# Attention with shared key heads on one core: VectorE's add and AND ahead of the copy of the transposes, and three-block jobs from the ninth on

## The chip, the core and the metric

The kernel runs on one core of a Trainium2 chip. The metric is the device time of one execution in microseconds (us). The engines have these names in the profile: PE is TensorE's matmul queue and PEld its weight loads, DVE is VectorE, ACT is ScalarE, POOL is GpSimd, SP is SyncE, which issues the stores.

## The reference

Q is (8, 512, 32, 64): batch, sequence, heads, head size. K and V are (8, 512, 8, 64): each of the 8 key heads serves 4 query heads.

```python
scores = np.einsum('bhqd,bhkd->bhqk', Q, K_expanded) * scale          # scale = 1/8
weights = np.exp(scores - np.max(scores, axis=-1, keepdims=True))
weights = weights / (np.sum(weights, axis=-1, keepdims=True) + 1e-10)
output = np.einsum('bhqk,bhkd->bhqd', weights, V_expanded)
```

The kernel leaves out the subtraction of the maximum and divides after the second product: a column of ones beside V gives the row sums. A flag computed from the sums and from V's largest value says at the end whether that was safe; a general path behind it runs only if it was not.

## The kernel before, in words

**Jobs.** The work is cut into 64 jobs, numbered j = 0 to 63. A job is one batch and one key head with its 4 query heads, held as 2 pairs (`NPAIR`; a pair's two heads lie in the two halves of the partitions, index m). Two jobs in a row (g = 0 and 1) share one load of Q, called u = j // 2. The scores of a job are 16 blocks, each of 128 keys by the 512 queries of one head: 2 pairs x 4 key chunks (kc) x 2 (m). The order of all instructions is written out by hand: each engine runs its own in the order in which the loop over j issues them.

**The exponential is shared out.** Most blocks go to ScalarE: `act_tile(j, n)` puts two blocks into a tile of PSUM (`s_ps`, two buffers) with two matmuls (L208) and turns them into f16 weights with one activation of 1024 columns (L226). The first two blocks of the second pair go to VectorE instead; in a wide job (`WIDE(j)`, taken(j) = 3) the first three do, and one ScalarE tile of the job then has only 512 columns. Either way a job has 7 activations. In the kernel before, the wide jobs are j = 10, 12, ... 62.

**VectorE's share of a job** is a chain over two jobs and two engines. `exp_d` (L237) writes the integer `u` from the scores in `d_ps`, `exp_d2` takes the low bits `f` with an AND (L258), GpSimd makes the correction in two instructions (`g`, L250, then `w`, L254), and in the next job `exp_d4` adds `u` and `w` into the weights `pt` (L271). `by_pool(j)`, true for j = 3 to 62, says that GpSimd makes the correction; for the other jobs VectorE does it all. The first two blocks of `u` are made at the head of the job itself, a third one at the end of the job ahead, in the second bank of the tile that holds the transposes.

**The d_ps tile.** The pool `dps` has one buffer of two banks. It is used twice per job: first for the two score blocks of `exp_d`, then, behind `norm(last, 0)`, for the transposes of Q for a later job (`trans_q`, 8 small matmuls on L172) in bank 0. In a wide job bank 1 then holds the half tile of ScalarE; in the first batch it holds the transposes of K (`first_k`). VectorE copies the transposes to SBUF (`qt`, L176, and `kt_first`, L146). The matmuls that write the next use of `d_ps` wait until the copy has read it. `apart` tells the framework that two accesses touch different banks of one tile, so that it puts no wait between them.

**Transposes ahead.** Job j transposes Q for j + 1 while j < 7; job 7 does so for 8 and 9, in the two banks, and later jobs for j + 2.

**The second product and the division.** Job j computes the second product of job j - 1 (`pv(last, ...)`, L302, 32 small matmuls per pair into a single-buffered `pv` tile), in pieces between the score tiles. Pair 0 comes first; `norm(last, 0)` divides (reciprocal L345, product with broadcast L349). Pair 1 may start when the division of pair 0 has read the `pv` tile; its `blocks` order is kc = 2, 3, 1, 0, so that VectorE's blocks (kc 0 and, in a wide job, the first of kc 1) come last. `cut` says where the pieces of pair 1 end: (11, 19) in a narrow job, (4, 18) in a wide one. Of VectorE's own order in a job, the part that matters is: `u`, for odd j the check of V (L182), division of pair 0, copy of the transposes, add, check of the sums (L313, in every eighth job), AND, third `u` block if the next job is wide, division of pair 1.

**Queues.** POOL issues the loads of Q, K and V (L126, L103, L111) at the head of a job, ahead of that job's correction. SP issues the stores and the transposing copies of K.

Of the kernel before, what the change touches and what calls it, by code (L numbers as in the profile page):

```python
# [33 lines left out]
V_HI = 1.0e15  # L34


WIDE = lambda j: j >= 10 and j % 2 == 0


@with_exitstack  # L40
# [18 lines left out]
def fast_path(ctx, tc, Q, K, V, out, flag):  # L59
    nc = tc.nc  # L60
# [39 lines left out]
    def load_k(b, lo=0, hi=KV):  # L100
        if b not in kn:
            kn[b] = knat_pool.tile([128, SC, KV, D], BF16, name="k_nat")
        nc.gpsimd.dma_start(  # L103
            out=kn[b][:, :, lo:hi, :],
            in_=K[b, :, lo:hi, :].rearrange("(sc p) g d -> p sc g d", p=128),
        )


    def load_v(b, lo=0, hi=KV, chunks=range(SC)):
        for sc in chunks:  # L110
            nc.gpsimd.dma_start(  # L111
                out=vt[b % 2][:, sc, lo:hi, 0:D],
                in_=V[b, sc * 128:(sc + 1) * 128, lo:hi, :],
            )
# [6 lines left out]
    def load_q(u, cuts=(0, 2 * HPG)):  # L121
        b, gp = divmod(u, GP)
        h0 = gp * 2 * HPG
        qn[u] = qnat_pool.tile([128, SC, 2 * HPG, D], BF16, name="q_nat")
        for lo, hi in zip(cuts[:-1], cuts[1:]):
            nc.gpsimd.dma_start(  # L126
                out=qn[u][:, :, lo:hi, :],
                in_=Q[b, :, h0 + lo:h0 + hi, :].rearrange("(sc p) h d -> p sc h d", p=128),
            )

    def d_tile():
        return d_pool.tile([128, 2, S], FP32, name="d_ps")
# [15 lines left out]
    def dma_k(b):  # L148
        kt[b] = kt_pool.tile([128, 2, GP, S], BF16, name="kt")
        for sc in range(SC):  # L150
            nc.sync.dma_start_transpose(
                out=kt[b][:, 0, :, sc * 128:(sc + 1) * 128],
                in_=kn[b][:, sc, :, :].rearrange("p g d -> p (g d)"),
            )
        for to, of in ((0, 64), (64, 0)):
            nc.sync.dma_start(out=kt[b][to:to + 64, 1, :, :], in_=kt[b][of:of + 64, 0, :, :])

    def apart(this, other):
        if other is not None:
            tc.declare_no_dep(  # L160
                this.ins, other.ins, reason="the two are in different banks of one tile"
            )
        return this

    def trans_q(j, bank, lo=0, hi=NPAIR, other=None):
        u, g = divmod(j, 2)
        ps = bank.bitcast(BF16).rearrange("p (i sc c) -> p i sc c", i=NPAIR, sc=SC)
        for i in range(lo, hi):
            for sc in range(SC):
                h = g * HPG + 2 * i  # L170
                apart(
                    nc.tensor.transpose(ps[:, i, sc, :], qn[u][:, sc, h:h + 2, :], ident), other  # L172
                )
        if u not in qt:
            qt[u] = qt_pool.tile([128, 2, NPAIR, S], BF16, name="qt")
        return lambda: apart(nc.vector.tensor_copy(  # L176
            out=qt[u][:, g, lo:hi, :], in_=ps[:, lo:hi, :, :].rearrange("p i sc c -> p i (sc c)")
        ), other)
# [11 lines left out]
    DPAIR = NPAIR - 1  # L190

    def taken(j):
        return 3 if WIDE(j) else 2

# [9 lines left out]
    def scores(j, ps, i, kc, m):  # L204
        u, g = divmod(j, 2)
        b, gp = divmod(u, GP)
        keys = kt_first[:, gp, :, :] if b == 0 else kt[b][:, :, gp, :]
        nc.tensor.matmul(  # L208
            ps,
            keys[64 * m:64 * m + 64, g ^ m, kc * 128:(kc + 1) * 128],  # L210
            qt[u][64 * m:64 * m + 64, g, i, :],
            start=True,
            stop=True,
        )

    def open_job(j):
        pt = pt_pool.tile([128, NPAIR, SC, 2, S], FP16, name="pt")
        jobs.setdefault(j, {}).update(pt=pt, pv={})

    def act_tile(j, n, spare=None):  # L220
        group = act_tiles(j)[n]
        i, kc, lo = group[0]
        ps = s_pool.tile([128, 2, S], FP32, name="s_ps") if spare is None else spare
        for _, _, m in group:
            scores(j, ps[:, m, :], i, kc, m)
        return nc.scalar.activation(  # L226
            out=jobs[j]["pt"][:, i, kc, lo:, :], in_=ps[:, lo:, :], func=EXP, scale=scale
        )

    def exp_d(j, lo, hi, ps):  # L230
        st = jobs.setdefault(j, {})
        if "u" not in st:
            for name, dtype in (("u", I16), ("f", I16), ("g", BF16), ("w", BF16)):
                st[name] = dve_pool.tile([128, 3, S], dtype, name=name + "16")[:, 0:taken(j), :]
        for n in range(lo, hi):
            scores(j, ps[:, n - lo, :], DPAIR, n // 2, n % 2)
        return lambda: nc.vector.tensor_scalar(  # L237
            out=st["u"][:, lo:hi, :], in0=ps[:, 0:hi - lo, :], scalar1=A_U, scalar2=B_U,
            op0=ALU.mult, op1=ALU.add,
        )  # L240


    def by_pool(j):
        return 3 <= j < NJOB - 1
# [23 lines left out]
    def exp_d4(j):  # L268
        st = jobs[j]
        n = taken(j)  # L270
        nc.vector.tensor_tensor(  # L271
            out=st["pt"][:, DPAIR, :, :, :].rearrange("p kc m q -> p (kc m) q")[:, 0:n, :].bitcast(
                U16
            ),
            in0=st["u"],
            in1=st["w"],
            op=ALU.add,
        )
# [132 lines left out]
    bank = d_tile()  # L411
# [4 lines left out]
    bank = d_tile()  # L416
# [3 lines left out]
    for j in range(NJOB):  # L420
        end = j == NJOB - 1
        last = j - 1
        late = last >= 0
        u, g = divmod(j, 2)
        b, gp = divmod(u, GP)
        open_job(j)
        if j == 1:

            nc.gpsimd.tensor_copy(out=gate, in_=jobs[0]["pt"][0:1, 0, SC - 1, 0, 0:1])
            load_q(2)  # L430
            load_q(3)
        if g == 0 and u >= 1 and u + 3 < NU:
            load_q(u + 3)
        if (gp, g) == (1, 0) and b + 1 < B:
            load_k(b + 1)
        if 3 <= 2 * gp + g < 3 + SC and b + 1 < B:
            load_v(b + 1, chunks=(2 * gp + g - 3,))
        if gp == 2 and g == 0 and b + 1 < B:
            dma_k(b + 1)

        cut = (4, 18) if taken(j) > 2 else (11, 19)
        act_tile(j, 0)
        if j == 0:
            trans_q(0, bank[:, 1, :], 1, NPAIR)()
            act_tile(j, 1)
            exp_d(j, 0, 2, d_tile())()
        else:
            exp_d(j, 0, 2, d_tile())()
            act_tile(j, 1)

        if j == 8:
            check_v(0, 0)
        if g == (b < B - 1) and j > 1:
            check_v(b, gp)
        if late:
            pv(last, 0, 0, 16)
        act_tile(j, 2)
        if late:
            pv(last, 0, 16, 32)
            norm(last, 0)  # L460
        act_tile(j, 3)

        reads = []
        if not end:
            bank = d_tile()
            beside = act_tile(j, 4, bank) if taken(j) > 2 else None

            ahead = (j + 1,) if j < 7 else (8, 9) if j == 7 else (j + 2,)
            for n, to in enumerate(ahead):
                if to < NJOB:  # L470
                    reads.append(trans_q(to, bank[:, n, :], other=beside))
            if j == 1:
                for swap in range(2):
                    reads.append(first_k(1, swap, bank[:, 1, swap * S // 2:]))
            elif j > 1 and b == 0 and gp + 1 < GP:
                reads.append(first_k(gp + 1, g, bank[:, 1, :]))
        else:
            pv(j, 0, 0, 16)
        for read in reads:
            read()  # L480

        if late and by_pool(last):
            exp_d4(last)
        check_sums()
        exp_d2(j)
        if not by_pool(j):
            exp_d3(j, nc.vector)
            exp_d4(j)
        if taken(j) == 2:
            act_tile(j, 4)  # L490
        if late:
            pv(last, 1, 0, cut[0])
        act_tile(j, 5)
        if not end and taken(j + 1) > 2:
            exp_d(j + 1, 2, taken(j + 1), bank[:, 1:2, :])()
        if late:
            pv(last, 1, *cut)
        act_tile(j, 6)
        if late:
            pv(last, 1, cut[1], 32)  # L500
            norm(last, 1)
            del jobs[last]
        if end:
            pv(j, 0, 16, 32)
            norm(j, 0)
            pv(j, 1, 0, 32)
            norm(j, 1)
# [118 lines left out]
```

## Time and profile before

| | |
|---|---|
| median of 3 runs | 422.61 us (421.35 to 422.84) |
| profiled execution | 421.88 us, of which the span from first to last instruction is 420.1 us |
| mean granted TensorE clock | 0.987 |
| busy shares | ACT 96%, PE 91%, DVE 83%, POOL 70% |
| ScalarE's exponentials on `s_ps` | 421 instructions of 1024 columns, 393.2 us busy |
| HBM traffic | 50.33 MB read, 33.55 MB written, 200 GB/s over the span |

Rows of the timeline read: start (us), duration (us), engine, line, operation, output tile <- input tiles, how many instructions the row joins, and in square brackets the idle time just before them with what ended it. Successive instructions of one kind are joined, so a row's duration can hold small gaps; activations overlap their successors, so starts say more than durations. The 7 activations of each job make the clock by which the loop can be followed: job 22 has its first at 150.93 us, job 23 at 156.84 us.

### The profile page before, as it was taken

The page shows a single profiled execution, that of the slowest core. Times are in us where ns is not written, and L with a number is a line of the kernel's source. Part 1 is how long each engine was busy: PE and PEld are TensorE (multiplying, and loading weights), DVE is VectorE, ACT ScalarE, POOL GpSimd, SP SyncE. Part 2 cuts the span into 40 slices and gives each one's busy share as a digit, 9 for nine tenths or more (in the row PEclk, how much of TensorE's full clock was granted, in tenths as well). Part 3 has the DMA queues.
Part 4 walks back from the last instruction along what each step waited for, and adds up shares of the span by engine and source line. Part 5 has one row for each costly group of instructions (what it writes and reads, how often), then busy time and mean ns, then how long its engine had stood idle before and what let it go on. Part 6 is the DMA issues. An engine that isn't in the chain of part 4 may idle for free.

```text
span 420.1 us, 13063 instructions
## 1 busy us (share of the span) xinstructions
PE 382.4 (91%) x5689; PEld 232.7 (55%) x5689; DVE 350.1 (83%) x611; ACT 402.2 (96%) x449; POOL 292.3 (70%) x209
## 2 busy tenths in 40 slices
PE   6889999999999999999999999999999999999993
PEld 2456565555555555555555555555555555555552
DVE  2697878888888888898888898888889888988875
ACT  3899999999999999999999999999999999999992
POOL 8504656689758886788866977778875888676560
PEclk9799999999999999999999999999999999999997
DMA  9996985499966998599983999649996799842223
GB/s 98 178 138 156 221 167 138 75 195 188 214 152 88 222 198 160 142 176 152 213 180 102 213 145 249 185 64 200 203 191 151 100 212 200 167 131 101 103 99 107
DMA packets 91438, 66.95 MB, mean 159 GB/s; under 512 B 52080, under 2 KB 74608, under 8 KB 91376
## 3 DMA queue, kind: packets, MB, share of 16 engines
q0 software_dynamic: 56544, 25.17, 52.6%
q1 hardware_dynamic: 34832, 40.90, 33.3%
q8 instruction: 45, 0.74, 0.7%
q14 instruction: 17, 0.14, 0.1%
HBM read 50.33 MB, written 33.55 MB: 200 GB/s over the span
## 4 chain that ended last, share of the span: by engine, by line
ACT 61%; PE 26%; DVE 9%; issue 1%; POOL 1%; ACTq 0%; DVEq 0%; POOLq 0%
ACT pt L226 61%; PE pv L302 11%; PE s_ps L208 10%; PE d_ps L172 3%; DVE o_sb L349 2%; DVE pt L271 2%; DVE u L237 1%; DVE ok L313 1%; PE d_ps L208 1%; DVE f L258 1%; DVE qt L176 1%; DVE w L254 1%; POOL q_nat L126 0%; DVE kt_first L146 0%; PE d_ps L143 0%
## 5 line engine op out<-in xcount | busy, mean ns | idle before, releaser
L226 ACT ACTIVATE pt<-s_ps 128x1024 f16<-128x1024 f32 x421 | 393.2, 1124 | 9.2 <-PE s_ps L208 9.1
L302 PEld LDWEIGHTS <-pt 128*128 128x128 f16 x4096 | 144.1, 98 | 87.8 <-issue 53.6
L302 PE MATMUL pv<-v,pt 128*128 128x65 bf16 x4032 | 183.4, 195 | 8.1 <-DVE pt L271 4.2
L254 POOL TENSOR_TENSOR w<-g,f 128x1024 bf16<-128x1024 bf16 (+1 forms) x60 | 153.9, 2565 | 5.0
L208 PE MATMUL s_ps<-qt,kt 64*128 64x512 bf16 x730 | 142.8, 384 | 15.1 <-ACT pt L226 9.7
L250 POOL TENSOR_SCALAR g<-f 128x1024 bf16<-128x1024 int16 (+1 forms) x60 | 74.0, 1234 | 107.4 <-DVE f L258 107.4
L237 DVE TENSOR_SCALAR u<-d_ps 128x1024 int16<-128x1024 f32 (+1 forms) x91 | 96.2, 1057 | 0.6 <-PE d_ps L208 0.6
L349 DVE TENSOR_TENSOR o_sb<-pv,inv 128x512 f32<-128x512 f32 x125 | 86.5, 692 | 4.5 <-DVE inv L345 0.2
L208 PEld LDWEIGHTS <-kt 64*128 64x128 bf16 x896 | 47.9, 93 | 55.4 <-issue 29.4
L345 DVE RECIPROCAL inv<-pv 128x8 f32<-128x8 f32 x125 | 25.9, 207 | 40.1 <-PE pv L302 39.7
L271 DVE TENSOR_TENSOR pt<-u,w 128x1536 uint16<-128x1536 int16 (+1 forms) x64 | 51.1, 799 | 4.7 <-POOL w L254 3.0
L176 DVE COPY qt<-d_ps 128x1024 bf16<-128x1024 bf16 (+1 forms) x65 | 44.3, 683 | 8.9 <-PE d_ps L172 6.9
L208 PE MATMUL d_ps<-qt,kt 64*128 64x512 bf16 x166 | 41.9, 375 | 0.3
L172 PE MATMUL d_ps<-ident,q_nat 128*128 128x128 bf16 x512 | 40.4, 223 | 1.0 <-DVE kt_first L146 0.9
L172 PEld LDWEIGHTS <-q_nat 128*128 128x128 bf16 x512 | 29.5, 99 | 20.9 <-issue 20.9
L258 DVE TENSOR_SCALAR f<-u 128x1536 int16<-128x1536 int16 (+1 forms) x64 | 30.8, 481 | 0.0
L111 POOL DMA_DIRECT2D v<-in_V_dram x32 | 29.0, 911 | 0.5 <-DMA v<-in_V_dram 0.5
L126 POOL DMA_DIRECT2D q_nat<-in_Q_dram x34 | 27.4, 808 | 1.8 <-DMA q_nat<-in_Q_dram 1.6
L208 PE MATMUL s_ps<-qt,kt_first 64*128 64x512 bf16 x112 | 23.0, 406 | 4.7 <-ACT pt L226 3.8
L182 DVE TENSOR_REDUCE okv<-v 128x1 f32<-128x512 bf16 x32 | 21.6, 676 | 0.0
L226 ACT ACTIVATE pt<-d_ps 128x512 f16<-128x512 f32 x27 | 18.5, 685 | 0.0
L208 PEld LDWEIGHTS <-kt_first 64*128 64x128 bf16 x128 | 7.9, 94 | 12.4 <-issue 8.5
(41 smaller groups left out, 45.3 us busy)
## 6 DMA issues: line engine op xcount, KB each, us to landing
out_dram<-o_sb SPq DMA_DIRECT2D x31, 1024.0 KB, 6.8
q_nat<-in_Q_dram POOLq DMA_DIRECT2D x31, 512.0 KB, 6.1
k_nat<-in_K_dram POOLq DMA_DIRECT2D x7, 512.0 KB, 8.7
v<-in_V_dram POOLq DMA_DIRECT2D x28, 128.0 KB, 7.2
kt<-kt SPq DMA_DIRECT2D x14, 256.0 KB, 4.8
out_dram<-o_sb SPq DMA_DIRECT2D x4, 256.0 KB, 2.4
kt<-k_nat SPq DMA_TRANSPOSE x28, 5.6
v<-in_V_dram POOLq DMA_DIRECT2D x4, 96.0 KB, 8.4
```

The source lines that it names most:

```text
L111: nc.gpsimd.dma_start(out=vt[b % 2][:, sc, lo:hi, 0:D], in_=V[b, sc * 128:(sc + 1) * 128, lo:hi, :],)
L172: nc.tensor.transpose(ps[:, i, sc, :], qn[u][:, sc, h:h + 2, :], ident), other
L176: return lambda: apart(nc.vector.tensor_copy(out=qt[u][:, g, lo:hi, :], in_=ps[:, lo:hi, :, :].rearrange("p i sc c -> p i (sc c)")), other)
L208: nc.tensor.matmul(ps, keys[64 * m:64 * m + 64, g ^ m, kc * 128:(kc + 1) * 128], qt[u][64 * m:64 * m + 64, g, i, :], start=True, stop=True,)
L226: return nc.scalar.activation(out=jobs[j]["pt"][:, i, kc, lo:, :], in_=ps[:, lo:, :], func=EXP, scale=scale)
L237: return lambda: nc.vector.tensor_scalar(out=st["u"][:, lo:hi, :], in0=ps[:, 0:hi - lo, :], scalar1=A_U, scalar2=B_U, op0=ALU.mult, op1=AL ...
L250: engine.tensor_scalar(out=g, in0=f, scalar1=-EXP_F1, scalar2=EXP_K * 2.0 ** (24 * as_bits), op0=ALU.add, op1=ALU.mult,)
L254: engine.tensor_tensor(out=w, in0=g, in1=f.bitcast(FP16) if as_bits else f, op=ALU.mult)
L258: nc.vector.tensor_single_scalar(out=st["f"], in_=st["u"], scalar=1023, op=ALU.bitwise_and)
L271: nc.vector.tensor_tensor(out=st["pt"][:, DPAIR, :, :, :].rearrange("p kc m q -> p (kc m) q")[:, 0:n, :].bitcast(U16), in0=st["u"], in1=st ...
L302: nc.tensor.matmul(st["pv"][i][:, m, qc, :], st["pt"][:, i, kc, m, qc * 128:(qc + 1) * 128], vt[b % 2][:, kc, 2 * gp + g, :], start=(n < 2 ...
L349: nc.vector.tensor_tensor(out=osb[u][:, :, h:h + 2, :].rearrange("p qc m d -> p m qc d"), in0=sums[:, :, :, 0:D], in1=inv[:, :, :, None].t ...
```

## The change

Four edits go together.

- `WIDE` begins at j = 8 instead of 10, so that job 8 is wide too: its third block is computed at the end of job 7.
- Job 6 transposes Q for jobs 7 and 8, and job 7 only for 9; before, job 6 did so for 7, and job 7 for 8 and 9. That leaves bank 1 free in job 7 for the third block of job 8.
- In the jobs with `by_pool(j)` the copies of the transposes move behind the add of the last job, the check of the sums and the AND of this job. In the other jobs (0 to 2 and 63) they stay where they were.
- The score matmul of the third block is declared apart from the copy of the transposes (`copies[0]`), which lies in the other bank; otherwise it would wait for that copy.

```diff
-WIDE = lambda j: j >= 10 and j % 2 == 0
+WIDE = lambda j: j >= 8 and j % 2 == 0
...
-        nc.tensor.matmul(
+        return nc.tensor.matmul(
...
-    def exp_d(j, lo, hi, ps):
+    def exp_d(j, lo, hi, ps, other=None):
...
         for n in range(lo, hi):
-            scores(j, ps[:, n - lo, :], DPAIR, n // 2, n % 2)
+            apart(scores(j, ps[:, n - lo, :], DPAIR, n // 2, n % 2), other)
...
-            ahead = (j + 1,) if j < 7 else (8, 9) if j == 7 else (j + 2,)
+            ahead = (j + 1,) if j < 6 else (7, 8) if j == 6 else (j + 2,)
...
-        for read in reads:
-            read()
-
+        copies = [] if by_pool(j) else [read() for read in reads]
         if late and by_pool(last):
             exp_d4(last)
         check_sums()
         exp_d2(j)
         if not by_pool(j):
             exp_d3(j, nc.vector)
             exp_d4(j)
+        else:
+            copies = [read() for read in reads]
...
-            exp_d(j + 1, 2, taken(j + 1), bank[:, 1:2, :])()
+            exp_d(j + 1, 2, taken(j + 1), bank[:, 1:2, :], copies[0])()
```

## The prediction

> **What bounds the kernel now.** I read the busy shares first, then the stretches of equal length, then ScalarE's timeline alone, then all engines over two jobs, and last the list of who waited for whom.
>
> ```profile
> PE 382.4 (91%) x5689; PEld 232.7 (55%) x5689; DVE 350.1 (83%) x611; ACT 402.2 (96%) x449; POOL 292.3 (70%) x209
> 160.00:210.00 50.00, 47.01 (x709) 28.44 (x708) 43.64 (x75) 49.99 (x57) 38.59 (x26) 1.00 0.96 169
> ```
>
> The second row is a stretch of 50 us: length, sum, then busy time of PE, PEld, DVE, ACT and POOL, granted clock, DMA share, GB/s. ScalarE is busy for 49.99 of 50 us at a clock of 1.00. Read as it stands, only less work for ScalarE could help. But its activations overlap, so a late start can hide in a longer busy time. The starts tell:
>
> ```profile
> 62.68 13.86 ACT L226 ACTIVATE pt<-s_ps 128x1024 f16<-128x1024 f32 x15
> 76.24 1.22 ACT L226 ACTIVATE pt<-s_ps 128x1024 f16<-128x1024 f32 x1
> 79.86 0.84 ACT L226 ACTIVATE pt<-d_ps 128x512 f16<-128x512 f32 x1
> 80.33 12.28 ACT L226 ACTIVATE pt<-s_ps 128x1024 f16<-128x1024 f32 x13
> 154.55 0.66 ACT L226 ACTIVATE pt<-d_ps 128x512 f16<-128x512 f32 x1
> 155.03 12.10 ACT L226 ACTIVATE pt<-s_ps 128x1024 f16<-128x1024 f32 x13
> 403.25 0.67 ACT L226 ACTIVATE pt<-d_ps 128x512 f16<-128x512 f32 x1
> 161.36 1.18 ACT L226 ACTIVATE pt<-s_ps 128x1024 f16<-128x1024 f32 x1
> 162.40 1.06 ACT L226 ACTIVATE pt<-s_ps 128x1024 f16<-128x1024 f32 x1
> ```
>
> From 62.68 to 76.24 us, 15 full tiles start 13.56/15 = 0.904 us apart: ScalarE's own pace. A half tile is followed after 0.48 us (154.55 to 155.03). So a wide and a narrow job together need 13 x 0.904 + 0.48 = 12.23 us. The half tiles mark these pairs: from 79.86 to 403.25 us there are 26 of them, 323.39/26 = 12.44 us each. So 0.206 us per pair, 26 x 0.206 = **5.36 us** in all, is time in which a full ScalarE had no tile ready. The place is the last tile of the narrow job: in job 23 it starts 162.40 - 161.36 = 1.04 us after the one before, 0.14 late. Why:
>
> ```profile
> 153.37 0.69 DVE L349 TENSOR_TENSOR o_sb<-pv,inv 128x512 f32<-128x512 f32 x1
> 154.21 0.69 DVE L176 COPY qt<-d_ps 128x1024 bf16<-128x1024 bf16 x1 [0.16 <-PE d_ps L172]
> 154.82 0.68 DVE L271 TENSOR_TENSOR pt<-u,w 128x1024 uint16<-128x1024 int16 x1
> 155.42 0.55 DVE L258 TENSOR_SCALAR f<-u 128x1536 int16<-128x1536 int16 x1
> 156.07 1.47 POOL L250 TENSOR_SCALAR g<-f 128x1536 bf16<-128x1536 int16 x1 [1.40 <-DVE f L258]
> 156.39 0.39 PE L208 MATMUL d_ps<-qt,kt 64*128 64x512 bf16 x2
> 157.62 3.10 POOL L254 TENSOR_TENSOR w<-g,f 128x1536 bf16<-128x1536 bf16 x1
> 159.27 0.69 DVE L349 TENSOR_TENSOR o_sb<-pv,inv 128x512 f32<-128x512 f32 x1
> 159.91 0.69 DVE L176 COPY qt<-d_ps 128x1024 bf16<-128x1024 bf16 x1
> 160.75 0.96 DVE L271 TENSOR_TENSOR pt<-u,w 128x1536 uint16<-128x1536 int16 x1 [0.15 <-POOL w L254]
> 161.28 0.32 PE L302 MATMUL pv<-v,pt 128*128 128x65 bf16 x5
> 161.63 0.42 DVE L258 TENSOR_SCALAR f<-u 128x1024 int16<-128x1024 int16 x1
> 161.77 0.27 PE L302 MATMUL pv<-v,pt 128*128 128x65 bf16 x3 [0.17 <-DVE pt L271]
> 161.96 0.68 DVE L237 TENSOR_SCALAR u<-d_ps 128x512 int16<-128x512 f32 x1
> 161.97 0.39 PE L208 MATMUL s_ps<-qt,kt 64*128 64x512 bf16 x2
> 162.89 0.21 DVE L345 RECIPROCAL inv<-pv 128x8 f32<-128x8 f32 x1 [0.24 <-PE pv L302]
> ```
>
> The chain runs AND of the wide job (155.42), POOL's two instructions (156.07 to 160.72), add in the narrow job (160.75), PE's three matmuls that use its result (161.77), and behind them on PE the scores of the last tile (161.97). How it looks without that wait, job 9 shows, which has the third block but no three-block add:
>
> ```profile
> 74.36 0.42 PE L302 MATMUL pv<-v,pt 128*128 128x65 bf16 x8
> 74.76 0.39 PE L208 MATMUL s_ps<-qt,kt 64*128 64x512 bf16 x2
> POOL g L250 <- DVE f L258: 107.4, 60, 17.3
> ```
>
> There the scores follow 0.40 us after the eight matmuls begin, and ScalarE keeps its pace. In job 23 they follow after 0.69. The last row says that POOL waited for the AND before each of its 60 jobs.
>
> **The change part by part.** *Add and AND ahead, wide job.* The add follows the division after 0.63 us (154.21 stands behind a wait; 159.27 to 159.91 gives 0.64), at 154.00 instead of 154.82. The AND keeps its 0.60 behind the add: 154.60, ended at 155.15. POOL begins 0.10 later as now (155.97 to 156.07), at 155.25: 0.82 earlier. Its w then ends at 159.90 instead of 160.72. The copy runs from 155.15 to 155.84, and PE's next write of d_ps at 156.39 keeps 0.55 us of reserve. The 0.16 that VectorE waited for the transposes is covered by the add.
>
> *Narrow job.* Division until 159.91, w at 159.90, so the add starts at about 159.94, 0.81 earlier, and PE, which reaches the three matmuls at 161.60, finds it done (160.90). The scores of the last tile start 0.29 earlier, and 0.14 is wanted: the gap closes with 0.15 left over. What is queued behind the add: AND 0.88 later (160.82), copy 0.33 later (161.15, until 161.84), third u block until about 162.5, then the reciprocal, which PE's product now asks for at 162.89 - 0.29 = 162.60. It fits with 0.1 us.
>
> *Check of the sums, every eighth job.*
>
> ```profile
> 174.02 0.61 DVE L313 SCALAR_TENSOR_TENSOR ok<-inv,ok 128x128 f32<-128x128 f32 x2
> 174.54 0.42 DVE L258 TENSOR_SCALAR f<-u 128x1024 int16<-128x1024 int16 x1
> 175.48 0.20 DVE L345 RECIPROCAL inv<-pv 128x8 f32<-128x8 f32 x1
> 185.72 0.96 DVE L271 TENSOR_TENSOR pt<-u,w 128x1536 uint16<-128x1536 int16 x1 [0.31 <-POOL w L254]
> 186.74 0.27 PE L302 MATMUL pv<-v,pt 128*128 128x65 bf16 x3 [0.32 <-DVE pt L271]
> ```
>
> The check (job 25) puts 0.52 us between add and AND, and two jobs later add and PE wait twice as long. VectorE's instructions in job 25 are the same number with one wait of about 0.15 fewer, so its reciprocal comes no later in relation to ScalarE; in job 27 the add comes 0.82 earlier as above against a wait of 0.32. I take these gaps as closed too, and leave 0.1 us of the 5.36 for crumbs. Part: **-5.26**.
>
> *Job 8 wide.* One full activation becomes a half one: 0.904 - 0.48 = **-0.42** on ScalarE. VectorE gets one more u (0.68) and a longer add and AND (0.28 and 0.13), POOL 0.4 + 1.0; a pair leaves VectorE (50 - 43.64)/50 x 12.4 = 1.6 us and POOL 2.8 us idle. Without that cover the same add would be late as in job 11.
>
> *Transposes moved.*
>
> ```profile
> 59.42 1.07 PE L172 MATMUL d_ps<-ident,q_nat 128*128 128x128 bf16 x16
> 60.53 1.29 DVE L176 COPY qt<-d_ps 128x1024 bf16<-128x1024 bf16 x2 [0.39 <-PE d_ps L172]
> ```
>
> The double portion takes 1.07 us of PE in job 7 and goes to job 6 whole; its price (at most 0.5, half of 1.07) moves with it: 0. *Jobs 3 to 9 otherwise, queues:* the waits from 33 to 79 us hold none of PE for the add; the loads on POOL keep their place ahead of the correction, SP's stores hang on the divisions: 0. *Apart:* the third block's matmul writes at once, as now: 0; with the wait it would hold PE until the copy at 161.84. *Job 63* keeps its order, so what lies behind ScalarE's last tiles moves with them.
>
> Sum: -5.26 - 0.42 = -5.7 against the execution's own 421.88 us gives 416.2. That execution lies 0.73 below the median of the runs; from the median it would be 416.9. I forecast **416.6**. Bounds of the unknown: the copy now runs beside POOL's g. The nearest row is the copy at 159.91 beside w, 0.69 as alone, so I take no stretch; a copy's length lost in POOL (0.69) would bring the add to 160.6, done at 161.5 and still ahead of 161.60.
>
> **The rivals.** *ScalarE is full (0.07).* If 49.99 of 50 busy means what it says, only job 8 counts: 421.88 - 0.42 = 421.5. The spacing of 1.04 against 0.904 with an equal busy time speaks against it. The Trainium skill, Trace Analysis, Identifying the Most-Contended Engine, takes busy share for ScalarE as a fair measure of the distance to the limit. By that rule the forecast would be this rival's; here the row of starts differs from it.
>
> *Half the gap stays (0.10).* The reserve of 0.15 at the last tile, or of 0.1 at the reciprocal, is too small in part of the pairs, and PE itself is next: 0.42 + 5.36/2 = 3.1, so 418.8. For it: PE is busy 47.01 of 50. Against: job 9's rows.
>
> *The add blocks VectorE (0.07), slower.* Place: the add in narrow jobs now stands ahead of AND, copy and third u. If POOL's w ends as late as now, the add stays at 160.75, AND 161.63, copy 161.96, u 162.57, reciprocal 163.25 instead of 162.89: 0.36 late, then the division and PE's next product. 26 x 0.36 - 0.42 = 8.9: 430.8 at most; with half of it absorbed 426. It decides from where w comes less than about 0.4 earlier. Against: POOL waits for the AND each time.
>
> ```profile
> 153.78 0.89 POOL L111 DMA_DIRECT2D v<-in_V_dram x1
> ```
>
> For it: in pairs with a V load, add and AND now meet POOL's issue (until 154.67) by 0.07. The Trainium skill, SBUF - State Buffer, Who interferes with whom, says that VectorE's two-port modes shut GpSimd out of a shared port for a whole instruction. No row shows an issue beside an AND; by that rule w would come some 0.1 later there, far from the 0.4 that decides.
>
> **How the numbers follow.** The forecast gets 0.73, with 415.4 to 417.8 as its own range (all gaps and half a microsecond at the start gained, or 1.2 left). Low 415.4; high 419.8 takes in the half gap and the scatter between runs. 0.03 stays for the unthought. About 0.5%, 2.1 us, is what a measurement can tell from no change. Faster: 0.73 + 0.10; same: 0.07 and the 0.03; slower 0.07.
>
> **What would show it.** Half tiles 12.23 to 12.3 us apart, the first in job 8; POOL's g about 1.9 us behind the division's start in wide jobs; no wait of PE for L271 in narrow ones; PE's d_ps matmuls not waiting for L176. Wrong would be: L271 waiting for POOL w by 0.4 us or more, the reciprocal of pair 1 late behind u, or a new wait of ScalarE at another tile.

## The result and the profile after

The changed kernel takes 420.62 us (median of 21 runs, 420.13 to 421.89) against 421.88 us before (21 runs, 421.31 to 422.98). The ratio is 0.9971, with a 95% interval of 0.9962 to 0.9981: 1.3 us faster (0.8 to 1.6). Forecast were 416.6 us and a saving of 5.7 us. The direction was right, four fifths of the gain did not come, and the time lies outside the range of 415.4 to 419.8.

VectorE and GpSimd did nearly what the working said, and the wait of TensorE for the add is gone. This is the timeline of the changed kernel over the same pair of jobs (22 and 23).

```profile
153.56 0.69 DVE L349 TENSOR_TENSOR o_sb<-pv,inv 128x512 f32<-128x512 f32 x1
154.17 0.68 DVE L271 TENSOR_TENSOR pt<-u,w 128x1024 uint16<-128x1024 int16 x1
154.77 0.55 DVE L258 TENSOR_SCALAR f<-u 128x1536 int16<-128x1536 int16 x1
155.24 0.68 DVE L176 COPY qt<-d_ps 128x1024 bf16<-128x1024 bf16 x1
155.42 1.47 POOL L250 TENSOR_SCALAR g<-f 128x1536 bf16<-128x1536 int16 x1 [1.39 <-DVE f L258]
156.97 3.10 POOL L254 TENSOR_TENSOR w<-g,f 128x1536 bf16<-128x1536 bf16 x1
...
159.54 0.69 DVE L349 TENSOR_TENSOR o_sb<-pv,inv 128x512 f32<-128x512 f32 x1
160.15 0.95 DVE L271 TENSOR_TENSOR pt<-u,w 128x1536 uint16<-128x1536 int16 x1
161.01 0.42 DVE L258 TENSOR_SCALAR f<-u 128x1024 int16<-128x1024 int16 x1
161.35 0.68 DVE L176 COPY qt<-d_ps 128x1024 bf16<-128x1024 bf16 x1
161.55 0.41 PE L302 MATMUL pv<-v,pt 128*128 128x65 bf16 x8
161.94 0.39 PE L208 MATMUL s_ps<-qt,kt 64*128 64x512 bf16 x2
```

GpSimd's g starts 1.86 us behind the wide job's division (forecast about 1.9). Its w ends at 160.07, ahead of the add, which waits for nothing. PE's eight matmuls run in one piece, and the scores follow 0.39 us after their start, as in job 9 of the kernel before. The page of the whole run says the same. Its rows for before come first, those of the changed kernel behind them:

```profile
L302 PE MATMUL pv<-v,pt 128*128 128x65 bf16 x4032 | 183.4, 195 | 8.1 <-DVE pt L271 4.2
L271 DVE TENSOR_TENSOR pt<-u,w 128x1536 uint16<-128x1536 int16 (+1 forms) x64 | 51.1, 799 | 4.7 <-POOL w L254 3.0
L226 ACT ACTIVATE pt<-s_ps 128x1024 f16<-128x1024 f32 x421 | 393.2, 1124 | 9.2 <-PE s_ps L208 9.1
```

```profile
L302 PE MATMUL pv<-v,pt 128*128 128x65 bf16 x4032 | 178.8, 195 | 2.4 <-DVE o_sb L349 1.9
L271 DVE TENSOR_TENSOR pt<-u,w 128x1536 uint16<-128x1536 int16 (+1 forms) x64 | 51.1, 799 | 0.2
L226 ACT ACTIVATE pt<-s_ps 128x1024 f16<-128x1024 f32 x420 | 398.1, 1284 | 9.7 <-PE s_ps L208 9.5
```

In the kernel before, PE lost 4.2 us here to the add and the add lost 3.0 us to w (the columns are busy time, mean ns | idle before, its releaser). Both are gone. But the last line of each shows something that nobody had asked for: the mean activation lasts 1284 ns where it lasted 1124, at the same work and nearly the same total time. ScalarE's timeline of the changed kernel, first and last half tile from job 10 on, and the last two tiles of job 23:

```profile
80.14 0.90 ACT L226 ACTIVATE pt<-d_ps 128x512 f16<-128x512 f32 x1
161.46 1.35 ACT L226 ACTIVATE pt<-s_ps 128x1024 f16<-128x1024 f32 x1
162.38 1.35 ACT L226 ACTIVATE pt<-s_ps 128x1024 f16<-128x1024 f32 x1
402.70 0.91 ACT L226 ACTIVATE pt<-d_ps 128x512 f16<-128x512 f32 x1
```

The last tile of the narrow job now starts 0.92 us after the one before, not 1.04: the gap is closed. And yet a pair takes 322.56/26 = 12.41 us instead of 12.44; the forecast said 12.23. The time that the gap took has come back as longer activations.

PE tells the same. Its scores of the last tile start at 161.94 us, where they started at 161.97 before: 0.03 us earlier, not 0.29. The reason lies ahead of the add, at a score tile of job 23 for which PE waits until ScalarE has read the buffer (before, then changed):

```profile
157.09 0.39 PE L208 MATMUL s_ps<-qt,kt 64*128 64x512 bf16 x2 [0.31 <-ACT pt L226]
157.36 0.39 PE L208 MATMUL s_ps<-qt,kt 64*128 64x512 bf16 x2 [0.31 <-ACT pt L226]
```

From there PE runs 0.27 us later, because the activation that it waits for ends 0.27 us later. From 60 to 400 us such waits of PE for ScalarE grew from 9.4 us in 33 places to 16.0 us in 55: what PE no longer waits for at the add, it waits for at the score tiles.

**Where it is.** The hint ahead of the profile, that starts say more than durations, misleads here. Take the ends instead of the starts. In the rows of before that stand in the prediction, the tile that ends the first row ends at 62.68 + 13.86 = 76.54, the next one at 76.24 + 1.22 = 77.46: 0.92 apart, though their starts keep 0.904. Around the gap in job 23 the ends lie at 162.54 and 163.46: 0.92 again. The tile that started 0.14 late lasted 1.06 us instead of 1.18. Over all 448 activations of either trace, an end follows the end before by 0.917 us (a half tile by 0.490; the expectations have 0.489) wherever ScalarE is fed. So its pace is 0.917, and a pair needs 13 x 0.917 + 0.490 = 12.41 us. Starts at 0.904 only mean that ScalarE takes in the next tile a little earlier each time: its lead over its own ends grows by 0.0125 us a tile, to be seen as a longer duration. A late start uses up the lead and costs nothing until it is gone. Where it was gone in the kernel before, the rows of job 27, a pair behind a check of the sums, show:

```profile
186.15 1.20 ACT L226 ACTIVATE pt<-s_ps 128x1024 f16<-128x1024 f32 x1
187.37 1.02 ACT L226 ACTIVATE pt<-s_ps 128x1024 f16<-128x1024 f32 x1
```

The first ends at 187.35, the second starts at 187.37 and is a fresh one of 1.02 us, ended at 188.39: 1.04 behind, 0.12 lost. Counted at the ends, from 75 to 400 us, before loses 0.65 us in all, in six such pairs of 0.07 to 0.13; after loses 0.00. With 0.43 for the half tile of job 8 that makes 1.08 us, within the interval of the 1.3 measured. The two profiled executions themselves are only 0.34 us apart (421.88 and 421.54 us): in the changed one the first activation ended 0.49 us later, and the first jobs lost some 0.3 us more.

### The profile page after: what moved, and what is told of

Its sections match the earlier page's. It is cut to its first block, busy times and chain, and to the rows that moved or that the text cites. A ratio compares the mean times of both kernels' runs of the same rounds, so it can differ in the third digit from the quotient of the medians.

```text
span 419.8 us, 13065 instructions
## 1 busy us (share of the span) xinstructions
PE 381.2 (91%) x5689; PEld 235.2 (56%) x5689; DVE 345.0 (82%) x612; ACT 401.3 (96%) x449; POOL 293.4 (70%) x209
## 4 chain that ended last, share of the span: by engine, by line
ACT 80%; PE 12%; DVE 5%; issue 1%; POOL 1%; ACTq 0%; DVEq 0%; POOLq 0%
ACT pt L226 80%; PE s_ps L208 6%; PE pv L302 3%; PE d_ps L172 1%; DVE o_sb L349 1%; DVE pt L271 1%; DVE qt L176 1%; DVE w L254 1%; POOL q_nat L126 0%; DVE u L237 0%; DVE kt_first L146 0%; PE d_ps L143 0%; DVE f L258 0%; DVE g L250 0%; PE d_ps L145 0%
## 5 line engine op out<-in xcount | busy, mean ns | idle before, releaser
L226 ACT ACTIVATE pt<-s_ps 128x1024 f16<-128x1024 f32 x420 | 398.1, 1284 | 9.7 <-PE s_ps L208 9.5
L302 PEld LDWEIGHTS <-pt 128*128 128x128 f16 x4096 | 142.6, 98 | 77.5 <-issue 56.3
L302 PE MATMUL pv<-v,pt 128*128 128x65 bf16 x4032 | 178.8, 195 | 2.4 <-DVE o_sb L349 1.9
L208 PEld LDWEIGHTS <-kt 64*128 64x128 bf16 x896 | 51.8, 93 | 62.3 <-issue 35.0
L208 PE MATMUL d_ps<-qt,kt 64*128 64x512 bf16 x168 | 43.0, 375 | 0.0
L226 ACT ACTIVATE pt<-d_ps 128x512 f16<-128x512 f32 x28 | 25.2, 899 | 0.0
L208 PEld LDWEIGHTS <-kt_first 64*128 64x128 bf16 x128 | 7.8, 95 | 12.3 <-issue 8.6
```

The lines of the kernel that those rows point to most:

```text
L208: return nc.tensor.matmul(ps, keys[64 * m:64 * m + 64, g ^ m, kc * 128:(kc + 1) * 128], qt[u][64 * m:64 * m + 64, g, i, :], start=True, st ...
L226: return nc.scalar.activation(out=jobs[j]["pt"][:, i, kc, lo:, :], in_=ps[:, lo:, :], func=EXP, scale=scale)
L302: nc.tensor.matmul(st["pv"][i][:, m, qc, :], st["pt"][:, i, kc, m, qc * 128:(qc + 1) * 128], vt[b % 2][:, kc, 2 * gp + g, :], start=(n < 2 ...
```

## The experiments

Two theories, named as in the expectations. S is the prediction's: the pace is 0.904 between starts, and each later start is lost. E: the pace is 0.917 between ends, and a start may be late by as much as the activation ahead is longer than a fresh one.

**One part at a time.** First the new order alone (all edits but the two on `WIDE` and `ahead`), then these two alone, with the old order.

```diff
-WIDE = lambda j: j >= 8 and j % 2 == 0
+WIDE = lambda j: j >= 10 and j % 2 == 0
...
-            ahead = (j + 1,) if j < 6 else (7, 8) if j == 6 else (j + 2,)
+            ahead = (j + 1,) if j < 7 else (8, 9) if j == 7 else (j + 2,)
```

> The new order on VectorE alone; three-block jobs from 10 on as before. Theory S (the prediction's: ScalarE's pace is the 0.904 us between starts, every later start is lost time): -5.3 us against before. Theory E (ScalarE's pace is the 0.917 us between ends; a late start costs nothing while the activations ahead have not ended): only the pairs with the check of the sums lose time at the ends, 0.07 to 0.12 us each, 0.65 us in all by the trace of before, so -0.65 us.

> Three-block jobs from 8 on and the transposes ahead, with the old order on VectorE. Theory S: -0.42 for the half tile, +0.2 for the gap that job 9 then gets, so -0.2 us. Theory E: one activation of 1024 columns becomes one of 512, 0.917 - 0.489 = 0.43 us at the ends, so -0.43 us, and e1 and e2 together give what the whole change gave.

Order alone: 421.31 us against 421.40 on the same chip, ratio 0.9992 (0.9981 to 1.0003), that is -0.8 to +0.1 us. S's 5.3 us are excluded; E's 0.65 lies inside, and so does no change at all. Wide alone: 421.31, ratio 0.9998 (0.9986 to 1.0011), -0.6 to +0.5 us, which holds both theories. Together the two ratios make 0.4 us, not the 1.3 of the whole change, as E expected; the interval of their sum, an estimate of -1.1 to +0.3 us from the two, overlaps with that of the whole change, so the times alone do not show how the gain is shared out. The traces are finer than the clock here: at the ends, from 75 to 400 us, the first loses 0.00 us, the second 0.57, before 0.65. So the order closes the few real losses, the wide job 8 does not.

**More work ahead of the gap.** In the kernel before, two activations per narrow job are split in halves:

```diff
+        if SPLIT(j, n):      # 11 <= j < 63 and j % 2 == 1 and n in (2, 3)
+            for m in range(2):
+                nc.scalar.activation(
+                    out=jobs[j]["pt"][:, i, kc, m, :], in_=ps[:, m, :], func=EXP, scale=scale
+                )
+            return None
         return nc.scalar.activation(
```

> The kernel before, with the activations of tiles 2 and 3 of each narrow job from 11 to 61 split into two of 512 columns (52 splits); they lie ahead of the gap in the starts. Theory S: a split costs 2 x 0.48 - 0.904 = 0.056 us, two of them 0.11, which lie in the gap of 0.14 that ScalarE waits for anyway: 0 to +0.3 us. Theory E: ScalarE has no gap; 52 x (2 x 0.489 - 0.917) = 52 x 0.061 = +3.2 us.

Measured: 424.03 us, ratio 1.0064 (1.0043 to 1.0085), +1.8 to +3.6 us. If ScalarE had waited 0.14 us in each narrow job, 0.11 us more work ahead of the wait would have been hidden. It was not: S falls, and E's 3.2 lies in the interval. E had left out that the losses behind the check go as well: the trace gives 3.3 us more work and 0.65 less lost at the ends, 2.6 as in the medians.

**The gap made again.** In the changed kernel the last tile of each narrow job starts later, because its scores are computed twice.

```diff
-        for _, _, m in group:
-            scores(j, ps[:, m, :], i, kc, m)
+        for _ in range(2 if 11 <= j < 63 and j % 2 == 1 and n == 6 else 1):
+            for _, _, m in group:
+                scores(j, ps[:, m, :], i, kc, m)
```

> The changed kernel, with the two score matmuls of the last tile of each narrow job from 11 to 61 issued twice into the same tile (the same result), so that 26 tiles start 0.2 to 0.3 us later. Theory S: each later start is lost, +5 to +8 us against the changed kernel (420.6), 426 to 429. Theory E: the activation ahead still has 1.35 - 1.02 = 0.33 us to run beyond a fresh one, so the late start is free: 420.6 to 421.1 us, that is -1.3 to -0.8 against before.

Measured: 420.90 us, inside E's 420.6 to 421.1; the ratio to before is 0.9989 (0.9976 to 1.0001), 0 to 1.0 us faster, which E's -1.3 to -0.8 overlaps only in part. S's 426 to 429 are excluded. Its timeline in job 23:

```profile
161.49 0.61 PE L208 MATMUL s_ps<-qt,kt 64*128 64x512 bf16 x4
161.06 1.29 ACT L227 ACTIVATE pt<-s_ps 128x1024 f16<-128x1024 f32 x1
162.13 1.14 ACT L227 ACTIVATE pt<-s_ps 128x1024 f16<-128x1024 f32 x1
```

Four score matmuls instead of two, and a start 1.07 us behind the last: a larger gap than the 1.04 that the prediction wanted to close. The ends lie at 162.35 and 163.27, 0.92 apart, and from 75 to 400 us nothing is lost. This settles it: gaps of this size in the starts were free.

**The check of the sums alone.** In the kernel before, the check moves behind the AND; it touches the very pairs that lost time.

```diff
-        check_sums()
         exp_d2(j)
+        check_sums()
```

> The kernel before, with only the check of the sums moved behind the AND (it touches 7 of the pairs); add, AND and copies keep their old order. Theory E: those pairs were the only ones that lost time, 0.65 us in all, and they then look like the others: -0.4 to -0.65 us, half of what the whole change gave. Theory S: 7 x (0.32 - 0.14) = -1.3 us, and the other 19 gaps of 0.14 stay worth having.

Both theories were wrong here: 427.29 us, ratio 1.0122 (1.0101 to 1.0143), 5 us slower. The timeline in job 25 and the waits from 60 to 400 us:

```profile
174.71 0.42 DVE L258 TENSOR_SCALAR f<-u 128x1024 int16<-128x1024 int16 x1
175.05 0.28 DVE L313 SCALAR_TENSOR_TENSOR ok<-inv,ok 128x128 f32<-128x128 f32 x1
175.22 1.05 POOL L250 TENSOR_SCALAR g<-f 128x1024 bf16<-128x1024 int16 x1 [1.42 <-DVE f L258]
175.37 1.03 DVE L313 SCALAR_TENSOR_TENSOR ok<-inv,ok 128x128 f32<-128x128 f32 x1
176.33 0.68 DVE L237 TENSOR_SCALAR u<-d_ps 128x512 int16<-128x512 f32 x1
```

```profile
PE d_ps L208 <- DVE u L237: 5.2, 7, 0.8
```

The two check instructions take 1.35 us instead of 0.61. The first, begun ahead of GpSimd's g, takes 0.28 us as in the kernel before; the second, begun behind it, takes 1.03 instead of 0.29 and ends 0.13 us after g does (176.40 against 176.27). The third u block comes late, PE waits up to 0.8 us for it in each of the 7 places, and ScalarE loses about 0.8 us in each of these pairs, real time at the ends: 5.4 us in all. The Trainium skill, SBUF - State Buffer, Who interferes with whom, says that a VectorE instruction with two inputs in SBUF contends with a GpSimd instruction that reads SBUF, and that the shared port is an exclusive lock. This trace agrees for the second check instruction: it reads two tensors in SBUF, and it ends only when g is done, in all 7 places. That g waits for the first one is not to be seen: g took its 1.05 us as before. So the check belongs ahead of the AND, where GpSimd is idle. The add, which also has two inputs in SBUF, stands there in both kernels.

**Less work for ScalarE.** If ScalarE alone sets the pace, more three-block jobs must save time.

```diff
-WIDE = lambda j: j >= 8 and j % 2 == 0
+WIDE = lambda j: j >= 8 and (j % 2 == 0 or j % 4 == 3) and j < 63    # e6
+WIDE = lambda j: 8 <= j < 63 and j % 8 != 1                           # e7
+WIDE = lambda j: 8 <= j < 63                                          # e8
```

> The changed kernel, with three-block jobs also at j = 11, 15, ... 59 (13 more). Theory E: ScalarE alone sets the pace, so each saves 0.43 us: -5.6 us against the changed kernel, 415.0, as long as VectorE (1.1 us more in each of 13 jobs, where a pair leaves it 1.6 us idle) and GpSimd keep up. Rival (ScalarE is not what limits; PE or VectorE is next): less than half of that, 418 or more.

> The changed kernel, with every job from 8 to 62 three blocks wide but those with the check of the sums (j = 9, 17, ...): 20 more. Theory E: -8.6 us against the changed kernel, 412.0, if nothing else becomes the limit. VectorE would be busy for about 96% there, so a part of it may be lost: 412 to 415. Rival (another engine limits): 416 or more.

> The changed kernel, with all jobs from 8 to 62 three blocks wide: 27 more. ScalarE alone would give -11.6 us, 409; VectorE would then need about 6.0 us of each job of 5.99 us and becomes the limit, so 411 to 415.

All three came out slower, by more with each further job: 428.16 (ratio 1.0149, 1.0129 to 1.0170), 433.53 (1.0270, 1.0246 to 1.0295) and 436.79 us (1.0350, 1.0330 to 1.0371). A new wait stood in the way. The timeline of the first:

```profile
78.85 0.90 ACT L226 ACTIVATE pt<-d_ps 128x512 f16<-128x512 f32 x1
79.80 0.37 PE L208 MATMUL d_ps<-qt,kt 64*128 64x512 bf16 x1 [0.58 <-ACT pt L226]
81.08 2.85 ACT L226 ACTIVATE pt<-s_ps 128x1024 f16<-128x1024 f32 x3 [0.41 <-PE s_ps L208]
```

Where a three-block job follows another, the third block's matmul writes the bank that ScalarE's half tile is still being read from. PE waits 0.58 us with all that is queued behind it, and ScalarE runs dry. Moved behind the next piece of the product, that matmul finds the bank free:

```diff
-        if not end and taken(j + 1) > 2:
+        third = not end and taken(j + 1) > 2
+        if third and taken(j) == 2:
             exp_d(j + 1, 2, taken(j + 1), bank[:, 1:2, :], copies[0])()
         if late:
             pv(last, 1, *cut)
+        if third and taken(j) > 2:
+            exp_d(j + 1, 2, taken(j + 1), bank[:, 1:2, :], copies[0])()
```

> As e6 (three-block jobs also at j = 11, 15, ... 59), but where a three-block job follows a three-block job, the matmul of its third block stands behind the second piece of the product of pair 1 instead of ahead of it. In e6 it waited 0.58 us there for ScalarE to read the half tile in the same bank, and ScalarE lost 0.52 at its last tile. Theory E: the wait is gone, 13 activations are halved, 13 x 0.43 = -5.6 us against the changed kernel: 415.0. Rival (PE or VectorE limits as soon as ScalarE has less to do): 418 or more.

> The same with every job from 8 to 62 but j = 9, 17, ... three blocks wide, 20 more than in the changed kernel. Theory E: -8.6 us, 412.0; VectorE is then busy for about 96%, so up to 3 us of it may be lost. Rival: 416 or more.

> The same with all jobs from 8 to 62, 27 more. ScalarE alone: -11.6 us, 409. VectorE's work in e8 was 45.2 of 50 us at 6.5 us a job, that is 5.88 us of the 5.99 that ScalarE would take: VectorE becomes the limit, 410 to 414.

Three of four: 418.74 us, ratio 0.9947 (0.9926 to 0.9968), faster than before; against the changed kernel (0.9971) the intervals overlap. ScalarE has 5.6 us less to do than in the changed kernel, and the trace finds 3.4 us lost at the ends from 75 to 400 us (0.00 in the changed kernel), so 2.2 should remain; the table further below shows 2.1, the ratios 1.0. Seven of eight: 425.30 us (1.0101, 1.0076 to 1.0125); all: 431.19 us (1.0235, 1.0210 to 1.0259). Against the expectation, VectorE's share is not what stops them: from 160 to 210 us it is busy for 44.94 and 45.05 of 50 us. The timeline of seven of eight:

```profile
110.22 0.96 DVE L271 TENSOR_TENSOR pt<-u,w 128x1536 uint16<-128x1536 int16 x1 [0.59 <-POOL w L254]
111.24 0.24 PE L302 MATMUL pv<-v,pt 128*128 128x65 bf16 x2 [0.47 <-DVE pt L271]
112.06 1.94 ACT L226 ACTIVATE pt<-s_ps 128x1024 f16<-128x1024 f32 x2 [0.56 <-PE s_ps L208]
```

With three blocks in nearly every job, GpSimd's w comes too late for the add, the add for PE, and PE for ScalarE: the chain that the prediction drew, only here it costs time: two such places in every eight jobs lose 0.67 us each at the ends, 1.3 of some 2.1 us. What makes up the rest, and the loss with all jobs wide, was not taken apart.

**A version between.** Only j = 11, 19, ... 59 are added to the three-block jobs (7), with the matmul moved as above.

```diff
+WIDE = lambda j: 8 <= j < 63 and (j % 2 == 0 or j % 8 == 3)
```

> As e9, with only j = 11, 19, ... 59 as further three-block jobs (7). In e9 a three-block job behind another took 0.15 us from ScalarE's lead over its own ends, and where a job with the check of the sums met a small lead, up to 0.27 us were lost at the ends. Here three jobs follow in which the lead can grow again by 0.0125 us a tile. Theory E: 7 x 0.43 = 3.0 us saved, about 0.07 lost in each eight jobs: -2.5 us against the changed kernel, 418.1, about as fast as e9 with half as many extra three-block jobs. Rival (every further three-block job costs more elsewhere than it saves): 420.5 or more.

Measured: 418.14 us, ratio 0.9929 (0.9908 to 0.9951): 3.0 us faster than before (2.1 to 3.9), faster than the changed kernel too (whose interval begins at 0.9962), and with the lowest ratio of all, though its interval overlaps with that of three of four. At the ends, 0.12 us are lost from 75 to 400 us, less than the 0.5 expected. From the ends 3.0 + 0.43 + 0.65 - 0.12 = 4.0 us were to be had against before, just above the measured 2.1 to 3.9. Some 0.3 of what is missing lies outside the span (2.0 us around it in most runs, 1.7 before). Its stretch from 160 to 210 us (columns as in the prediction):

```profile
160.00:210.00 50.00, 47.03 (x711) 28.67 (x709) 44.33 (x77) 50.00 (x58) 40.78 (x26) 1.00 0.91 171
```

VectorE and GpSimd are busier than before (43.64 and 38.59), ScalarE is as full, and what it no longer does is saved.

**Between the same two tiles.** The executions also differ ahead of the jobs that the change touches: in the 14 traces the first tile of job 4 ends anywhere between 37.00 and 39.65 us. Why, no run shows. From there on the traces can be compared tile by tile, from the end of the first tile of job 4 to that of job 10 (job 8 lies between), and from there to that of job 62:

| kernel | job 4 to 10 (us) | job 10 to 62 (us) |
|---|---|---|
| before | 38.58 | 323.22 |
| order alone (e1) | 38.58 | 322.57 |
| wide alone (e2) | 38.16 | 323.14 |
| changed | 38.16 | 322.57 |
| changed, 26 late starts (e4) | 38.16 | 322.57 |
| three of four (e9) | 38.16 | 320.49 |
| five of eight (e12) | 38.16 | 319.70 |

The order saves 0.65 us behind job 10, job 8 saves 0.42 ahead of it, and the changed kernel has both: 1.07 us. The 26 late starts of e4 cost nothing to the hundredth. In e12 the second stretch is 3.52 us shorter than before, and 7 x 0.427 + 0.65 - 0.12 gives 3.52: theory E accounts for all of it. Behind the second stretch the kernels of the table need 19.4 to 19.5 us each, so in these executions all other differences lie ahead of job 4 or outside the span.

## Why the prediction was wrong, point by point

- **What bounds the kernel: wrong, and the step that failed.** "ScalarE's own pace" was read from the starts as 0.904 us. The runs show 0.917 from end to end (e3: 52 more instructions cost what the ends say; e4: 26 later starts cost nothing). So "a full ScalarE had no tile ready" for 5.36 us was false; 0.65 us of it was real. The sign stood in rows that the prediction itself quoted: a duration of 1.22 us at 76.24, and 1.18 ahead of the late start against 1.06 behind it, though all three tiles are alike.
- **The chain of waits: right up to the add.** AND, g, w and add came as worked out, with w 0.65 us earlier instead of 0.82, because in the changed kernel the division itself came 0.19 later. The wait of PE's three matmuls disappeared. But the last scores came 0.03 us earlier instead of 0.29, since PE waits for ScalarE ahead of them: the add was not on the path. None of the three named signs of being wrong (a long wait of the add for w, a late reciprocal, a new wait of ScalarE) appeared; only the distance of the half tiles, 12.41 us instead of 12.23 to 12.3, told.
- **Add and AND ahead, -5.26: mis-sized.** It measured 0.65 us in the traces; e1's own interval is -0.8 to +0.1 us.
- **The pairs with the check: right in kind.** From 75 to 400 us they are the only ones with a loss at the ends, and it went. Their 0.32 of gap was 0.07 to 0.13 of loss.
- **Job 8 wide, -0.42: right.** The ends give 0.917 - 0.490 = 0.43, and from job 4 to job 10 the table above shows 0.42 us less in each kernel with job 8 wide. The interval of e2 is too wide to show it in the times; e12, with 7 more such steps, is 1.8 us (0.9971 against 0.9929) faster than the changed kernel where 3.0 were worked out.
- **Transposes moved, loads, apart, job 63: 0, as forecast.** The start gap of job 7 went to job 6, 0.09 at the ends against 0.08.
- **No stretch of the copy beside g: right.** It lasted 0.68 us, against 0.69 before.
- **The rivals.** "ScalarE is full" (0.07) was the true one: -0.42 and the little of the check pairs. The rule of the Trainium skill, Perfetto Trace Analysis, Identifying the Most-Contended Engine, that stood beside it, agrees with the result, and the row of starts that was held against it was misread. "Half the gap stays" did not occur: the gap in the starts closed, and closing it was worth little. "The add blocks VectorE" did not occur either.

## What to carry to other kernels

What follows is shown for ScalarE alone. Take its pace from the distance between the ends of its instructions, and see whether durations grow from one to the next: growing durations mean that it takes in work faster than it finishes it, and a late start there costs nothing until the duration has fallen to that of a fresh instruction. An engine that is busy for 50.00 of 50 us may well be full; before a wait elsewhere is priced, ask whether the full engine had run dry at its ends. Then take work from that engine, and look first for the wait that the moved work creates: here one matmul in the wrong place turned a gain of 2.2 us (e9) into a loss of 6.3 (e6), both against before.

## What the runs showed of the hardware

- Activations of 1024 columns from PSUM end 0.917 us apart and may start 0.904 apart; those of 512 end 0.490 apart. Two halves cost 0.06 us more than a whole (e3). Why starts and ends differ, no run shows.
- The duration of an activation is no price: 1.02 us fresh, up to 1.36 us with the queue ahead of it, at the same throughput.
- The check of the sums on VectorE took 0.61 us with GpSimd idle and 1.35 us beside GpSimd's g (e5), all of the difference in the instruction that began behind g, while g kept its 1.05; the copy out of PSUM was as long beside g as without.
